# A transformer block's first stage: load order, look-ahead and ring of the adaLN modulation, its column sums by transposes, and the row scale applied once

## The chip, the cores and the metric

The kernel runs on one core of a Trainium2 chip. TensorE (PE) multiplies, VectorE (DVE) and ScalarE (ACT) do elementwise work, SyncE (SP) and GpSimd (POOL) issue DMA transfers from device memory. Each engine takes its instructions in the order in which the program lists them and waits on semaphores of the others. The metric is the device time of one execution in microseconds (us), lower is better; a kernel's time is the median of its runs.

## What is computed

One block of a diffusion transformer on 256 tokens `x` and 256 context tokens `ctx`, width 2048. What the change touches is its opening: two conditioning vectors are turned into a shift and a scale per column, the RMS-normed inputs are modulated by them, and the result is multiplied by the projection matrix.

```python
def adaln(cond, w, b):
    mod = jax.nn.silu(cond) @ w + b
    return mod.reshape(cond.shape[0], N_MOD, D_MODEL)

def modulate(x, gain, shift, scale):
    return rms_norm(x, gain) * (1 + scale[:, None, :]) + shift[:, None, :]
...
        mod_x = adaln(c, w_ada[l], b_ada[l])
        mod_c = adaln(c_ctx[None, :], w_ada[l], b_ada[l])
        pc = split_projection(modulate(ctx, norm1_g[l], mod_c[:, 0], mod_c[:, 1]) @ w_in[l])
        px = split_projection(modulate(x, norm1_g[l], mod_x[:, 0], mod_x[:, 1]) @ w_in[l])
```

Behind it come a gated linear recurrence in two directions, windowed attention, a merge and a feed-forward layer with a convolution. The change leaves those as they are.

## The kernel before

All activations lie transposed, 128 columns of the width on the partitions and 512 tokens (256 of `x`, 256 of `ctx`) along the free axis; the width is 16 such k-tiles (`KT`). `xraw` holds the raw inputs, `hl` the modulated ones, split into a high part `xhi` and a remainder `xlo` in the fast matmul format (fp32r), since every product is made as three fp32r products, high by high, high by low and low by high (`mm3`). Weights arrive as 512 KB pieces in `raw` (four buffers), ACT casts them to `whi` (L110), DVE takes the remainder `wlo` (L111).

**Head.** The modulation comes in eight *chunks* of two k-tiles; a chunk needs eight 512 KB pieces of the adaLN weight. They land in eight ring slots, four in the tile `ringv`, four in `ringq` (these are buffers of later stages that are still free). SP issues chunk 0's pieces with the four 1 MB loads of `xraw` among them, then those of chunk 1. ACT squares each k-tile of `xraw` (L203), PE adds the squares over the partitions with a matrix of ones (`bankm<-t,cst`), and ACT makes the row scale `rs` of it (L140, L141).

**One chunk.** `ada_mm` multiplies the conditioning vectors `csr` (32 columns, two of them used) with the pieces, in plain f32: 16 matmuls of 32x512 per chunk, and the k-th writes to the 32 output partitions 32*(k mod 4), so four neighbours use four different groups of the array's columns. The four partial sums lie on 128 partitions of one bank. `mod_chunk` copies that bank to `rows` (ACT, L180), and four small matmuls with a 0/1 matrix `sel` turn each 128-column piece upright and add the four partials (`banks<-sel,t`). DVE makes `bcol` and `acol`, shift and scale per column, out of it (L185 to L187). Then for each of two k-tiles: DVE multiplies `xraw` by `rs` (L190), ACT applies scale and shift, 256 tokens at a time (L193), ACT casts to `xhi` (L130), DVE takes `xlo` (L131).

**The loop.** `for j in range(8)`: iteration j multiplies the two k-tiles of chunk j with the value weights (`unit_v_mm`, 24 products, `bankm<-whi,hl` and `bankm<-wlo,hl`, inputs stationary) and with three tiles of the forget-gate weights (`unit_f_mm`, 18 products, `banks<-hl,whi` and so on). Among them it makes the modulation of chunk j+2: half of its `ada_mm` behind the value products, half behind the gate products, then `mod_chunk(j + 2)`. After the loop come the heads of q (`q_heads`), whose low products are 128x256, and the rest of the kernel.

What sets the order on each engine is a list scheduler that runs when the program is built: it starts from the order of the code, shifted by the priorities (`tc.high_priority`), and lets an instruction pass another when its own estimate says that the other isn't ready. The result is fixed; on the chip each engine keeps to it.

Of the kernel before, what the change touches and what calls it, by code (L numbers as in the profile page):

```python
# [27 lines left out]
RUSH = 120  # L28
# [23 lines left out]
def block_kernel(ctx, tc, xct, prm, cst, ada2, wst, out):  # L52
    nc = tc.nc
    V, S, PE = nc.vector, nc.scalar, nc.tensor

    cons = ctx.enter_context(tc.tile_pool(name="cons", bufs=1))
    big = ctx.enter_context(tc.tile_pool(name="big", bufs=1))
    strm = ctx.enter_context(tc.tile_pool(name="strm", bufs=3))
    scr = ctx.enter_context(tc.tile_pool(name="scr", bufs=3))
    tiny = ctx.enter_context(tc.tile_pool(name="tiny", bufs=8))  # L60
    mm = ctx.enter_context(tc.tile_pool(name="mm", bufs=5, space=bass.MemoryType.PSUM))
    ms = ctx.enter_context(tc.tile_pool(name="ms", bufs=3, space=bass.MemoryType.PSUM))

    def bank(pool=None):
        pool = pool or mm
        return pool.tile([P, 512], F32, name="bank" + ("m" if pool is mm else "s"))

    def mmul(o, l, r, start, stop):
        PE.matmul(o, l, r, start=start, stop=stop, skip_group_check=True)  # L69
# [69 lines left out]
    def rsqrt(dst, src, scale):  # L139
        S.activation(dst, src, AF.Ln, bias=eps_c, scale=scale)  # L140
        S.activation(dst, dst, AF.Exp, scale=-0.5)  # L141
# [22 lines left out]
    sel = smalltile(2, "sel")  # L164
    V.tensor_tensor(sel, ident[:, 0:2], ident[:, 32:34], op=ALU.add)
    V.tensor_tensor(sel, sel, ident[:, 64:66], op=ALU.add)
    V.tensor_tensor(sel, sel, ident[:, 96:98], op=ALU.add)
    rs = scr.tile([P, 512], F32, name="rs", bufs=1)

    def ada_load(i):  # L170
        st.load_raw(slots[i])

    def ada_mm(aps, half):
        for kt in range(8 * half, 8 * half + 8):
            g = 32 * (kt % 4)
            mmul(aps[g:g + 32, :], csr[:, kt, :], slots[kt // 2][:, kt % 2 * 512:kt % 2 * 512 + 512], kt < 4, kt >= KT - 4)

    def mod_chunk(j, aps):
        rows = scr.tile([P, 512], F32, name="t")
        S.copy(rows, aps)  # L180
# [4 lines left out]
        V.tensor_tensor(bcol[:, js, :], a4[:, 0:2, :], bsh[:, js, None].broadcast_to([P, 2, 2]), op=ALU.add)  # L185
        V.tensor_tensor(acol[:, js, :], a4[:, 2:4, :], bsc[:, js, None].broadcast_to([P, 2, 2]), op=ALU.add)
        V.tensor_tensor(acol[:, js, :], acol[:, js, :], par("n1g")[:, js, None].broadcast_to([P, 2, 2]), op=ALU.mult)  # L187
        for kt in range(2 * j, 2 * j + 2):
            hn = scr.tile([P, 512], F32, name="t")
            V.tensor_tensor(hn, xraw[:, kt, :], rs, op=ALU.mult)  # L190
            for cnd in range(2):
                sl = slice(T * cnd, T * cnd + T)
                S.activation(hn[:, sl], hn[:, sl], AF.Identity, bias=bcol[:, kt, cnd:cnd + 1],  # L193
                             scale=acol[:, kt, cnd:cnd + 1])
            split(xhi[:, kt, :], xlo[:, kt, :], hn)

    ssq = bank()

    def x_part(i):
        nc.sync.dma_start(xraw[:, 4 * i:4 * i + 4, :], xct[:, 4 * i:4 * i + 4, :])  # L200
        for kt in range(4 * i, 4 * i + 4):
            sq = scr.tile([P, 512], F32, name="t")
            S.activation(sq, xraw[:, kt, :], AF.Square)  # L203
            mmul(ssq, ones, sq, kt == 0, kt == KT - 1)

    for i in range(8):
        ada_load(i)
        if i % 2:
            x_part(i // 2)
    for j in range(2):  # L210
        if j:
            for i in range(8):
                ada_load(i)
        aps = bank(ms)
        for half in range(2):
            ada_mm(aps, half)
        with tc.high_priority(offset=0 if j else RUSH):
            if not j:
                rsqrt(rs, ssq, 1.0 / D)
            mod_chunk(j, aps)  # L220
    base[0] = tc.tile_snap_priority()
    early_v = [bank() for _ in range(4)]

# [19 lines left out]
    def unit_v(j):  # L243
        st.load()
        return [st.next(4) for _ in range(2)]

    def unit_v_mm(j, wv, tts):
        for tt in tts:
            ts = slice(tt * P, tt * P + P)
            for k2 in range(2):  # L250
                kt = 2 * j + k2
                mm3(early_v[tt], xhi[:, kt, ts], xlo[:, kt, ts], *wv[k2], kt == 0, kt == KT - 1)

    def unit_f(j):
        st.load(6)
        w = [st.next() for _ in range(6)]
        st.pos = 8
        return w

    def unit_f_mm(j, w):  # L260
        for b in range(3):
            for k2 in range(2):
                kt = 2 * j + k2
                mm3(early_f[b], *w[3 * k2 + b], xhi[:, kt, :], xlo[:, kt, :], kt == 0, kt == KT - 1)


    for j in range(8):
        more = j < 6
        aps = bank(ms) if more else None
        wv = unit_v(j)  # L270
        if more:
            for i in range(4):
                ada_load(i)
        unit_v_mm(j, wv, range(4))
        if more:
            ada_mm(aps, 0)
        w = unit_f(j)
        if more:
            for i in range(4, 8):
                ada_load(i)  # L280
        unit_f_mm(j, w)
        if more:
# [243 lines left out]
    kT = big.tile([P, 2, 512], F32, name="kT", tag="kT")  # L526
    va = big.tile([P, 4, 256], F32, name="va", tag="va")
# [50 lines left out]
    for h in range(H):  # L578
        if h == 4:
            bs = [bank() for _ in range(4)]  # L580
# [4 lines left out]
        if h == 6:  # L585
            bs = [bank() for _ in range(4)]
# [384 lines left out]
```

## Time and profile before

| | |
|---|---|
| Median of three runs | 1745.06 us (1742.27 to 1748.81) |
| The profiled execution's own time | 1748.49 us |
| Its span, first to last instruction | 1746.6 us |
| PE busy | 1719.9 us, 98% of the span |
| DVE, ACT, POOL busy | 1197.0, 847.6, 68.4 us |
| Mean granted TensorE clock | 0.996 of full |
| Bytes moved by DMA | 371.85 MB, mean 213 GB/s |

In rows of the timeline the first number is the start in us from the span's beginning, the second the time from the first start to the last end of the row's instructions, then engine, line, operation, what is written from what is read, shape, and how many instructions the row holds. A bracket at the end is the engine's idle time before the row and what ended it. A plain f32 matmul shows as two records (x8 is four matmuls), an fp32r product as one. In rows that give busy time by stretches, (x..) is the count, then PEclk is the granted clock, then the share of the DMA engines that was busy, then GB/s.

### The profile page before, as it was taken

The page shows a single profiled execution, that of the slowest core. Times are in us where ns is not written, and L with a number is a line of the kernel's source. Part 1 is how long each engine was busy: PE and PEld are TensorE (multiplying, and loading weights), DVE is VectorE, ACT ScalarE, POOL GpSimd, SP SyncE. Part 2 cuts the span into 40 slices and gives each one's busy share as a digit, 9 for nine tenths or more (in the row PEclk, how much of TensorE's full clock was granted, in tenths as well). Part 3 has the DMA queues.
Part 4 walks back from the last instruction along what each step waited for, and adds up shares of the span by engine and source line. Part 5 has one row for each costly group of instructions (what it writes and reads, how often), then busy time and mean ns, then how long its engine had stood idle before and what let it go on. Part 6 is the DMA issues. An engine that isn't in the chain of part 4 may idle for free.

```text
span 1746.6 us, 24907 instructions
## 1 busy us (share of the span) xinstructions
PE 1719.9 (98%) x9562; PEld 1451.9 (83%) x9562; DVE 1197.0 (69%) x1807; ACT 847.6 (49%) x1292; POOL 68.4 (4%) x132
## 2 busy tenths in 40 slices
PE   7999999999999999999999999999999999999999
PEld 2567888888888888888888898888888888888887
DVE  1335967464669878697878797788766656666665
ACT  4335554252545755454455475555555334554332
POOL 0000100000000001010100000000000000000000
PEclk9999999999999999999999999999999999999999
DMA  9795744433436558686876567677755555555554
GB/s 374 297 364 184 265 143 157 161 117 117 136 104 214 202 189 289 233 309 237 304 249 231 190 215 256 228 239 262 233 183 186 188 185 188 183 192 182 190 196 145
DMA packets 103432, 371.85 MB, mean 213 GB/s; under 512 B 11280, under 2 KB 13712, under 8 KB 102800
## 3 DMA queue, kind: packets, MB, share of 16 engines
q1 hardware_dynamic: 84880, 303.14, 49.2%
q0 software_dynamic: 18432, 67.12, 11.8%
q8 instruction: 75, 1.23, 0.3%
q14 instruction: 45, 0.37, 0.1%
HBM read 368.11 MB, written 2.10 MB: 212 GB/s over the span
## 4 chain that ended last, share of the span: by engine, by line
PE 93%; DMA 4%; DVE 1%; issue 1%; ACT 0%; SPq 0%; DVEq 0%; POOLq 0%
PE bankm L69 84%; PE banks L69 6%; DMA araw<-in_ada_dram 3%; DVE wlo L111 1%; PE banks L493 0%; DMA raw<-in_wst_dram 0%; DVE acc L309 0%; DMA xraw<-in_xct_dram 0%; PE banks L666 0%; PE banks L317 0%; PE banks L485 0%; PE banks L475 0%; PE banks L522 0%; ACT whi L110 0%; PE banks L636 0%
## 5 line engine op out<-in xcount | busy, mean ns | idle before, releaser
L69 PE MATMUL bankm<-hl,whi 128*128 128x512 f32 (+1 forms) x3392 | 1163.3, 394 | 0.0
L69 PE MATMUL bankm<-hl,wlo 128*128 128x256 f32 (+2 forms) x3104 | 899.7, 290 | 4.1 <-DVE wlo L111 4.1
L111 DVE TENSOR_TENSOR wlo<-raw,whi 128x1024 fp32r<-128x1024 f32 x498 | 606.7, 1219 | 337.2 <-ACT whi L110 335.1
L110 ACT CAST whi<-raw 128x1024 fp32r<-128x1024 f32 x498 | 520.2, 1045 | 634.8 <-PE bankm L69 492.5
L69 PEld LDWEIGHTS bankm<-hl,whi 128*128 128x128 f32 x3392 | 633.0, 188 | 144.1
L69 PEld LDWEIGHTS bankm<-hl,wlo 128*128 128x128 f32 x3104 | 587.6, 189 | 16.4 <-DVE wlo L111 5.7
L309 DVE SCALAR_TENSOR_TENSOR acc<-araw,csil,acc 128x1024 f32<-128x1024 f32 x120 | 153.7, 1281 | 29.4 <-DMA araw<-in_ada_dram 28.6
L69 PE MATMUL bankm<-whi,hl 128*128 128x512 f32 x512 | 167.3, 400 | 6.3 <-ACT whi L110 6.3
L69 PEld LDWEIGHTS bankm<-whi,hl 128*128 128x128 f32 x512 | 96.7, 190 | 31.3 <-ACT whi L110 7.2
L304 POOL DMA_DIRECT2D araw<-in_ada_dram x128 | 68.2, 533 | 1172.5 <-DVE acc L309 671.7
L69 PE MATMUL bankm<-wlo,hl 128*128 128x512 f32 x256 | 101.2, 395 | 0.0
L69 PE MATMUL bankm<-yb,whi 128*128 128x512 f32 x256 | 91.0, 400 | 0.0
L69 PE MATMUL bankm<-g,whi 128*128 128x512 f32 x256 | 90.5, 399 | 0.0
L69 PE MATMUL bankm<-yb,wlo 128*128 128x256 f32 x256 | 72.2, 282 | 0.0
L69 PE MATMUL bankm<-g,wlo 128*128 128x256 f32 x256 | 71.9, 281 | 0.0
L813 DVE SCALAR_TENSOR_TENSOR xm<-bankm,modv,xm 128x256 f32<-128x256 f32 x96 | 46.4, 484 | 31.2 <-PE bankm L69 29.4
L69 PEld LDWEIGHTS bankm<-g,whi 128*128 128x128 f32 x256 | 48.1, 188 | 12.0
L69 PEld LDWEIGHTS bankm<-yb,whi 128*128 128x128 f32 x256 | 48.1, 188 | 11.8
L69 PEld LDWEIGHTS bankm<-wlo,hl 128*128 128x128 f32 x256 | 48.6, 190 | 10.6 <-DVE wlo L111 1.2
L69 PEld LDWEIGHTS bankm<-yb,wlo 128*128 128x128 f32 x256 | 48.4, 189 | 0.3
L69 PEld LDWEIGHTS bankm<-g,wlo 128*128 128x128 f32 x256 | 48.4, 189 | 0.0
L793 ACT ACTIVATE fs<-fs,prm 128x256 f32<-128x256 f32 x44 | 26.5, 601 | 43.7 <-DVE fs L368 43.5
(200 smaller groups left out, 1187.4 us busy)
## 6 DMA issues: line engine op xcount, KB each, us to landing
raw<-in_wst_dram SPq DMA_DIRECT2D x490, 512.0 KB, 3.4
araw<-in_ada_dram POOLq DMA_DIRECT2D x128, 512.0 KB, 4.7
ringv<-in_wst_dram SPq DMA_DIRECT2D x32, 512.0 KB, 5.9
ringq<-in_wst_dram SPq DMA_DIRECT2D x32, 512.0 KB, 6.3
xraw<-in_xct_dram SPq DMA_DIRECT2D x4, 1024.0 KB, 12.8
raw<-in_wst_dram SPq DMA_DIRECT2D x8, 384.0 KB, 7.3
xm<-in_xct_dram SPq DMA_DIRECT2D x2, 1024.0 KB, 9.1
out_dram<-xm SPq DMA_DIRECT2D x3, 512.0 KB, 3.6
```

Of the source, the lines that this page charges most:

```text
L69: PE.matmul(o, l, r, start=start, stop=stop, skip_group_check=True)
L110: S.copy(hi, raw)
L111: self.last = V.tensor_tensor(lo, raw, hi.bitcast(F32), op=ALU.subtract)
L304: nc.gpsimd.dma_start(raw, ada2[idx])
L309: V.scalar_tensor_tensor(acc, raw, csil[:, kt, 0:1], acc, op0=ALU.mult, op1=ALU.add)
L793: S.activation(t, s, AF.Identity, bias=cb[:, f:f + 1], scale=cw[:, f, 1:2])
L813: V.scalar_tensor_tensor(xm[:, j, :], o[:, T * i:T * i + T], gate2[:, j:j + 1], xm[:, j, :], op0=ALU.mult, op1=ALU.add)
```

## The change

Five edits, all in the head and in the loop over eight chunks.

- **Loads.** The four loads of `xraw` come first, then only chunk 0's eight pieces, then the value and gate weights of iteration j ahead of the pieces of chunk j+1.
- **Look-ahead.** The head makes one chunk (0) instead of two. Iteration j makes chunk j+1: the first half of its `ada_mm` behind the value products, the second half behind the first of the three gate tiles, then `mod_chunk(j + 1)` at a raised priority, then the other two gate tiles.
- **Ring.** Three groups of four slots in place of two: `ringv`, `ringq`, and a spare group in two buffers of a later stream (`araw`) and two further tiles (`ringkT`, `ringva`). Half h of chunk j uses group (2j+h) mod 3.
- **Column sums.** The four matmuls with `sel` become four 128x128 transposes (L181), and one DVE reduction adds the four partials (L183).
- **Row scale.** All 16 k-tiles of `xraw` are multiplied by `rs` in place, once, in the head (L214). Per k-tile ACT then writes `xhi` straight from `xraw` (L192, 256 tokens at a time), DVE makes the same value in f32 in place (L193) and takes `xlo` (L194). The separate cast to `xhi` is gone.

```diff
-    slots = [r[:, i, :] for r in ring for i in range(4)]
+    spare = [strm.tile([P, 1024], F32, name="araw", bufs=2) for _ in range(2)]
+    spare += [big.tile([P, 1024], F32, name="ring" + t, tag=t) for t in ("kT", "va")]
+    slots = [[r[:, i, :] for i in range(4)] for r in ring] + [spare]
...
+    def ada_load(j, half):
+        for slot in slots[(2 * j + half) % 3]:
+            st.load_raw(slot)
...
         for q in range(4):
-            mmul(aps[:, 2 * q:2 * q + 2], rows[:, q * P:q * P + P], sel, q == 0, True)
-        a4 = aps[:, 0:8].rearrange("p (q c) -> p q c", c=2)
+            PE.transpose(aps[:, q * P:q * P + P], rows[:, q * P:q * P + P], ident)
+        m8 = smalltile(8).rearrange("p (q c) -> p q c", c=2)
+        V.tensor_reduce(m8, aps.rearrange("p (q g c) -> p q c g", q=4, g=4)[:, :, 0:2, :], axis=AX.X, op=ALU.add)
...
         for kt in range(2 * j, 2 * j + 2):
-            hn = scr.tile([P, 512], F32, name="t")
-            V.tensor_tensor(hn, xraw[:, kt, :], rs, op=ALU.mult)
             for cnd in range(2):
-                sl = slice(T * cnd, T * cnd + T)
-                S.activation(hn[:, sl], hn[:, sl], AF.Identity, bias=bcol[:, kt, cnd:cnd + 1],
-                             scale=acol[:, kt, cnd:cnd + 1])
-            split(xhi[:, kt, :], xlo[:, kt, :], hn)
+                xs = xraw[:, kt, T * cnd:T * cnd + T]
+                a, b = acol[:, kt, cnd:cnd + 1], bcol[:, kt, cnd:cnd + 1]
+                S.activation(xhi[:, kt, T * cnd:T * cnd + T], xs, AF.Identity, bias=b, scale=a)
+                V.tensor_scalar(xs, xs, a, b, op0=ALU.mult, op1=ALU.add)
+            V.tensor_tensor(xlo[:, kt, :], xraw[:, kt, :], xhi[:, kt, :].bitcast(F32), op=ALU.subtract)
...
-    for i in range(8):
-        ada_load(i)
-        if i % 2:
-            x_part(i // 2)
-    for j in range(2):
...
+    for i in range(4):
+        x_part(i)
+    aps = bank(ms)
+    for half in range(2):
+        ada_load(0, half)
+        ada_mm(aps, 0, half)
+    with tc.high_priority(offset=RUSH):
+        rsqrt(rs, ssq, 1.0 / D)
+        for kt in range(KT):
+            V.tensor_tensor(xraw[:, kt, :], xraw[:, kt, :], rs, op=ALU.mult)
+        mod_chunk(0, aps)
...
     for j in range(8):
-        more = j < 6
+        wv, w = unit_v(j), unit_f(j)
+        more = j < 7
         aps = bank(ms) if more else None
...
+        for half in range(2 * more):
+            ada_load(j + 1, half)
         unit_v_mm(j, wv, range(4))
         if more:
-            ada_mm(aps, 0)
...
+            ada_mm(aps, j + 1, 0)
+        unit_f_mm(j, w, (0,))
         if more:
-            ada_mm(aps, 1)
-            mod_chunk(j + 2, aps)
+            ada_mm(aps, j + 1, 1)
+            with tc.high_priority(offset=24):
+                mod_chunk(j + 1, aps)
+        unit_f_mm(j, w, (1, 2))
```

The host packs the weights in the new order, and both kernels issue the same number of matmuls for products and modulation. From six products ahead of the end of the loop on, PE's list is the same in both kernels; DVE's and ACT's differ up to the first heads of the recurrence and are the same from there.

On PE, before, around the end of one iteration and the start of the next (the first five iterations read so): `ringq,csr` is the second half of a chunk's modulation, `whi,hl` and `wlo,hl` are value products of the next iteration, `sel,t` the column sums.

```order
L69 MATMUL bankm<-hl,wlo 128x512
L69 MATMUL banks<-ringq,csr 32x512 x8
L69 MATMUL bankm<-whi,hl 128x512
L69 MATMUL bankm<-wlo,hl 128x512
L69 MATMUL bankm<-whi,hl 128x512 x2
L69 MATMUL banks<-sel,t 128x2 x4
```

Eight modulation matmuls stand together, and the chunk that is summed here is used a whole iteration later. The same place in the changed kernel, from the end of iteration 4 on (the modulation's pieces lie in `ringkT` and `ringva` here; `hl,whi` and `hl,wlo` are the last gate products of the iteration, `cst,t` are the transposes):

```order
L69 MATMUL banks<-ringkT,csr 32x512 x2
L69 MATMUL banks<-hl,whi 128x512
L69 MATMUL banks<-hl,wlo 128x512
L69 MATMUL bankm<-hl,whi 128x512
L69 MATMUL banks<-ringva,csr 32x512 x2
L69 MATMUL bankm<-hl,whi 128x512
L69 MATMUL bankm<-hl,wlo 128x512
L69 MATMUL bankm<-hl,whi 128x512 x2
L181 MATMUL banks<-cst,t 128x128 x4
L69 MATMUL bankm<-hl,wlo 128x512
L69 MATMUL bankm<-whi,hl 128x512 x2
L69 MATMUL bankm<-wlo,hl 128x512 x2
```

The modulation now stands in pieces of one to four matmuls with products between them, and one product behind the transposes the next iteration's value products begin, which read the very chunk that is being summed. From its first value product to the first 128x256 product of `q_heads`, PE's list of before holds 92 modulation matmuls in 12 runs (one of 4, eleven of 8); that of the change holds 111 in 32 runs: 7, 8, 8, 8, 2, 6, 6, 2, and then four times 1, 3, 4, 4, 2, 2.

On DVE, the head of the change (the first k-tiles of `xlo` follow further down; L226 and L227 are small steps of the gate's lower bounds):

```order
L214 TENSOR_TENSOR xraw<-xraw,rs 128x512 x16
L183 TENSOR_REDUCE tn<-banks 128x8
L226 TENSOR_TENSOR tn<-prm 128x16
L111 TENSOR_TENSOR wlo<-raw,whi 128x1024
L185 TENSOR_TENSOR acol<-tn,bsc 128x4
L187 TENSOR_TENSOR bcol<-tn,prm 128x4
L227 TENSOR_TENSOR tn<-prm,tn 128x16
L186 TENSOR_TENSOR acol<-acol,prm 128x4
```

Before, the three small steps L185 to L187 came first and two k-tiles of L190 behind them; now all 16 row-scale passes and one weight remainder stand ahead of chunk 0's shift and scale. On SP, the first loads of the change:

```order
L82 DMA prm<-in_prm_dram 128x635
L83 DMA cst<-in_cst_dram 128x256
L199 DMA xraw<-in_xct_dram 128x2048 x4
L117 DMA ringv<-in_wst_dram 128x1024 x4
L117 DMA ringq<-in_wst_dram 128x1024 x4
L109 DMA raw<-in_wst_dram 128x1024
```

Before, 22 pieces of the modulation and the four loads of `xraw` stood ahead of the first `raw`; now eight pieces do.

More of the change, by code (lines that the diff above doesn't have):

```diff
@@ L162, in block_kernel, with ada_mm @@
     V.tensor_copy(csr[:, :, 0:2], csil)
[L164 to L167, printed above, removed]
     rs = scr.tile([P, 512], F32, name="rs", bufs=1)
-    def ada_load(i):
-        st.load_raw(slots[i])
-    def ada_mm(aps, half):
+    def ada_load(j, half):
+        for slot in slots[(2 * j + half) % 3]:
+            st.load_raw(slot)
+    def ada_mm(aps, j, half):
         for kt in range(8 * half, 8 * half + 8):
-            g = 32 * (kt % 4)
-            mmul(aps[g:g + 32, :], csr[:, kt, :], slots[kt // 2][:, kt % 2 * 512:kt % 2 * 512 + 512], kt < 4, kt >= KT - 4)
+            g, c = 32 * (kt % 4), kt % 2 * 512
+            mmul(aps[g:g + 32, :], csr[:, kt, :], slots[(2 * j + half) % 3][kt % 8 // 2][:, c:c + 512], kt < 4, kt >= KT - 4)
     def mod_chunk(j, aps):
@@ L181, in mod_chunk @@
         for q in range(4):
-            mmul(aps[:, 2 * q:2 * q + 2], rows[:, q * P:q * P + P], sel, q == 0, True)
-        a4 = aps[:, 0:8].rearrange("p (q c) -> p q c", c=2)
+            PE.transpose(aps[:, q * P:q * P + P], rows[:, q * P:q * P + P], ident)
+        m8 = smalltile(8).rearrange("p (q c) -> p q c", c=2)
+        V.tensor_reduce(m8, aps.rearrange("p (q g c) -> p q c g", q=4, g=4)[:, :, 0:2, :], axis=AX.X, op=ALU.add)
         js = slice(2 * j, 2 * j + 2)
-        V.tensor_tensor(bcol[:, js, :], a4[:, 0:2, :], bsh[:, js, None].broadcast_to([P, 2, 2]), op=ALU.add)
-        V.tensor_tensor(acol[:, js, :], a4[:, 2:4, :], bsc[:, js, None].broadcast_to([P, 2, 2]), op=ALU.add)
+        V.tensor_tensor(acol[:, js, :], m8[:, 2:4, :], bsc[:, js, None].broadcast_to([P, 2, 2]), op=ALU.add)
         V.tensor_tensor(acol[:, js, :], acol[:, js, :], par("n1g")[:, js, None].broadcast_to([P, 2, 2]), op=ALU.mult)
+        V.tensor_tensor(bcol[:, js, :], m8[:, 0:2, :], bsh[:, js, None].broadcast_to([P, 2, 2]), op=ALU.add)
         for kt in range(2 * j, 2 * j + 2):
-            hn = scr.tile([P, 512], F32, name="t")
-            V.tensor_tensor(hn, xraw[:, kt, :], rs, op=ALU.mult)
             for cnd in range(2):
-                sl = slice(T * cnd, T * cnd + T)
-                S.activation(hn[:, sl], hn[:, sl], AF.Identity, bias=bcol[:, kt, cnd:cnd + 1],
-                             scale=acol[:, kt, cnd:cnd + 1])
-            split(xhi[:, kt, :], xlo[:, kt, :], hn)
+                xs = xraw[:, kt, T * cnd:T * cnd + T]
[3 more added lines that the diff above has]
+            V.tensor_tensor(xlo[:, kt, :], xraw[:, kt, :], xhi[:, kt, :].bitcast(F32), op=ALU.subtract)
     ssq = bank()
@@ L204, in x_part @@
             mmul(ssq, ones, sq, kt == 0, kt == KT - 1)
-    for i in range(8):
-        ada_load(i)
-        if i % 2:
-            x_part(i // 2)
-    for j in range(2):
[L211 to L220, printed above, removed]
+    for i in range(4):
[9 more added lines that the diff above has]
+        mod_chunk(0, aps)
     base[0] = tc.tile_snap_priority()
@@ L258, in unit_f, with unit_f_mm @@
         return w
-    def unit_f_mm(j, w):
-        for b in range(3):
+    def unit_f_mm(j, w, bs):
+        for b in bs:
             for k2 in range(2):
@@ L921 @@
     first = np.stack([fft[0], fbt[0], fft[1]], 0).transpose(1, 0, 2, 3)
-    parts = [ada1[0], ada1[1]]
+    parts = [ada1[0]]
     for j in range(8):
-        more = ada1[j + 2] if j < 6 else ada1[0:0, 0]
-        parts += [vh[0, j][None], more[0:4]]
         t6 = first[2 * j:2 * j + 2].reshape(6, P, P)
-        parts += [_halves(np, np.concatenate([t6, np.zeros((2, P, P), np.float32)], 0)), more[4:8]]
+        parts += [vh[0, j][None], _halves(np, np.concatenate([t6, np.zeros((2, P, P), np.float32)], 0))]
+        if j < 7:
+            parts.append(ada1[j + 1])
     parts.append(_halves(np, qt))
```

9 lines of the change are left out of this document (removed).

## The prediction

> **What bounds the kernel now.** I read the page first (busy shares, then the chain that ended last), then busy time by stretches cut at the first product of the loop over chunks (47.7 us) and at its end (157.7 us), then the timeline of the first 80 us.
>
> ```profile
> span 1746.6 us, 24907 instructions
> PE 1719.9 (98%) x9562; PEld 1451.9 (83%) x9562; DVE 1197.0 (69%) x1807; ACT 847.6 (49%) x1292; POOL 68.4 (4%) x132
> PE 93%; DMA 4%; DVE 1%; issue 1%; ACT 0%; SPq 0%; DVEq 0%; POOLq 0%
> ```
>
> PE is the bound: 98% busy, and 93% of the chain that ended last is its own work. So a change pays if it starts PE's long run earlier or takes work off PE, and costs if it gives PE more to do or lets it wait.
>
> ```profile
> 0.00:47.70 47.70, 31.06 (x121) 10.88 (x121) 7.96 (x31) 21.77 (x39) 0.20 (x4) 0.98 0.96 378
> 47.70:157.70 110.00, 109.26 (x569) 73.69 (x570) 39.27 (x67) 43.12 (x68) 0.66 (x1) 0.98 0.76 283
> 157.70:215.00 57.30, 55.42 (x326) 48.13 (x326) 52.01 (x84) 33.98 (x57) 6.33 (x12) 0.97 0.75 254
> 215.00:1746.60 1531.60, 1524.17 (x8550) 1319.20 (x8548) 1097.71 (x1629) 748.75 (x1130) 61.21 (x115) 1.00 0.59 201
> ```
>
> The columns are stretch, length, then busy time of PE, PEld, DVE, ACT, POOL, clock, DMA share, GB/s. The head is bound by DMA: 96% of the engines busy, 378 GB/s, PE idle for 16.6 us. The loop is bound by PE: 109.26 of 110.00 us busy, with DMA at 76%. Behind the loop PE's list is unchanged and PE idles for 1.9 and 7.4 us, so what the loop's end gains or loses, the kernel's end gains or loses. Two questions remain: when does the first product of the loop start, and how long does the loop take?
>
> **The head.** These rows carry it:
>
> ```profile
> 9.93 1.67 ACT L203 ACTIVATE t<-xraw 128x512 f32<-128x512 f32 x3 [5.16 <-DMA xraw<-in_xct_dram]
> 10.61 5.74 PE L69 MATMUL bankm<-t,cst 128*128 128x512 f32 x8 [1.56 <-ACT t L203]
> ...
> 31.11 0.69 ACT L140 ACTIVATE rs<-bankm,prm 128x512 f32<-128x512 f32 x1 [1.95 <-PE bankm L69]
> ...
> 32.63 0.63 ACT L141 ACTIVATE rs<-rs 128x512 f32<-128x512 f32 x1
> ...
> 34.35 1.29 DVE L190 TENSOR_TENSOR t<-xraw,rs 128x512 f32<-128x512 f32 x2
> ...
> 38.56 0.42 SPq L109 DMA_DIRECT2D raw<-in_wst_dram  x1
> ...
> 46.59 1.04 ACT L110 CAST whi<-raw 128x1024 fp32r<-128x1024 f32 x1 [2.72 <-DMA raw<-in_wst_dram]
> 47.66 1.23 DVE L111 TENSOR_TENSOR wlo<-raw,whi 128x1024 fp32r<-128x1024 f32 x1 [3.08 <-ACT whi L110]
> ...
> 47.69 1.22 PE L69 MATMUL bankm<-whi,hl 128*128 128x512 f32 x2 [6.32 <-ACT whi L110]
> ```
>
> The first weight is issued at 38.56 us, behind 22 modulation pieces, lands at 46.59, and PE starts at 47.69 after 6.32 us of waiting. The change puts eight pieces ahead of that weight: with the inputs 9.4 MB, 25 us at 378 GB/s. So the weight is no longer late. Next late is the chain from the inputs to chunk 0. The first input load had a 0.52 MB piece ahead of it; without that it lands 1.4 us earlier, first square at 8.5, first sum on PE at 9.2. The first four sums take 5.74 us (to 14.9); the other twelve take 3.63 us per four (22.74 to 26.37 in the rows below), to 25.8. L140 and L141 take 0.69 and 0.63: `rs` at 27.2. Chunk 0's pieces (8.85 MB, 23.4 us of transfer) and its 16 matmuls end at about 30, so they are not late. But DVE now makes all 16 row-scale passes first. Two take 1.29 us, so 16 take 10.3: 37.6. Then L183 (taken as 0.2), the weight remainder that stands before the shift and scale (1.23), the small steps to ACT's start (0.45, rows below) and ACT's first 256 tokens (1.58 for three, 0.53): the first product starts at 40.0. **Gain 7.7 us.** Bounds: 6.3 if the inputs land no earlier than before; 15.7 if the row-scale passes were off the path (a rival).
>
> **The modulation's matmuls.** On PE a product's pace, and what an interruption by modulation costs:
>
> ```profile
> 150.26 0.39 PE L69 MATMUL bankm<-wlo,hl 128*128 128x512 f32 x1
> 150.49 0.62 PE L69 MATMUL bankm<-whi,hl 128*128 128x512 f32 x2
> 150.94 0.39 PE L69 MATMUL bankm<-wlo,hl 128*128 128x512 f32 x1
> ```
>
> ```profile
> 55.40 0.39 PE L69 MATMUL bankm<-whi,hl 128*128 128x512 f32 x1
> 55.72 1.07 PE L69 MATMUL banks<-ringv,csr 128*32 128x512 f32 x8
> 56.72 0.73 PE L69 MATMUL banks<-hl,whi 128*128 128x512 f32 x2
> 57.28 0.39 PE L69 MATMUL banks<-hl,wlo 128*128 128x512 f32 x1
> ```
>
> ```profile
> 75.38 0.39 PE L69 MATMUL bankm<-hl,wlo 128*128 128x512 f32 x1
> 75.69 1.92 PE L69 MATMUL banks<-ringq,csr 128*32 128x512 f32 x16
> 77.55 0.50 PE L69 MATMUL bankm<-whi,hl 128*128 128x512 f32 x1
> 77.89 0.40 PE L69 MATMUL bankm<-wlo,hl 128*128 128x512 f32 x1
> ```
>
> Three products take 0.68 us, 0.227 each. From 55.40 to 57.28 lie three products and a run of four modulation matmuls: 1.88 - 0.68 = 1.20 us for the run. From 75.38 to 77.89 lie two products and a run of eight: 2.51 - 0.45 = 2.06. What does a run of fewer than four cost? Two places in the head tell it:
>
> ```profile
> 21.76 1.05 PE L69 MATMUL banks<-ringq,csr 128*32 128x512 f32 x4
> 22.74 3.70 PE L69 MATMUL bankm<-t,cst 128*128 128x512 f32 x8
> ...
> 26.37 1.06 PE L69 MATMUL banks<-ringq,csr 128*32 128x512 f32 x8
> 27.37 3.70 PE L69 MATMUL bankm<-t,cst 128*128 128x512 f32 x8
> ```
>
> Two matmuls (x4 records) hold PE for 0.98 us, four for 1.00. Neighbours that write to different groups of 32 partitions run side by side, so a run costs by rounds of four, begun ones included. That speaks against the change, whose order cuts the runs up. Before: one run of four and eleven of eight, 1.20 + 11 x 2.06 = 23.9 us. After: six runs of 6 to 8, two rounds each (12.4), and 26 of at most four, taken at 1.20 like the run of four (31.2): 43.6. **Cost 19.7 us**, of which 4.1 is the chunk that moved from the head into the loop. A single matmul shows nowhere; if short runs cost the 1.00 of the head rows, the term is 14.5.
>
> **The column sums.**
>
> ```profile
> 78.60 0.95 PE L69 MATMUL banks<-sel,t 128*128 128x2 f32 x8
> 79.41 0.47 PE L69 MATMUL bankm<-wlo,hl 128*128 128x512 f32 x1
> ...
> 137.08 1.05 PE L69 MATMUL banks<-sel,t 128*128 128x2 f32 x8 [0.71 <-ACT t L180]
> ...
> 269.33 0.27 PE L475 MATMUL banks<-cst,hb 128*128 128x128 f32 x1
> 269.44 0.27 PE L317 MATMUL banks<-cst,acc 128*128 128x128 f32 x1
> ```
>
> The four `sel` matmuls cost 0.81 us, six times in the loop, with one wait of 0.71: 5.6 us. Transposes of this shape start 0.11 us apart; four take 0.44, between that and 0.81 with a change of format, and I take 0.6, seven times: 4.2. **Gain 1.4 us.** The Trainium skill (TensorE: Matmul & The Clock Gate, Part 4: PE-mode transpose) gives some 275 ns for a transpose in a kernel. The row's duration agrees (0.27) but its spacing is 0.11; by 275 ns in sequence the seven groups would cost about 4.6 us more by my estimate, and the sum would be 1765. The trace decides for the spacing.
>
> **The wait that is new.** Before, a chunk was ready an iteration ahead. Now, in the last four iterations with modulation, the transposes stand one product from the iteration's end, and the next product reads the chunk.
>
> ```profile
> 40.17 0.15 DVE L185 TENSOR_TENSOR bcol<-banks,prm 128x4 f32<-128x4 f32 x1
> ...
> 40.42 0.16 DVE L187 TENSOR_TENSOR acol<-acol,prm 128x4 f32<-128x4 f32 x1
> ...
> 40.62 1.58 ACT L193 ACTIVATE t<-t,bcol,acol 128x256 f32<-128x256 f32 x3 [1.82 <-DVE acol L187]
> ```
>
> ```profile
> L318 DVE TENSOR_REDUCE modv<-banks 128x4 f32<-128x512 f32 x16 | 10.9, 684 | 8.6 <-PE banks L317 8.6
> ```
>
> From the first transpose: the fourth ends at 0.6; 0.1 to DVE; the reduction of 32 elements, between a tiny step (0.15) and the 512 of L318 (0.68), taken as 0.2; the small steps 0.45; ACT's first 256 tokens 0.53: `xhi` at 1.9. PE is through at 0.6 + 0.23. It waits 1.1 us, with the whole of its list queued behind. Four times: **cost 4.4 us** (up to 6.3 with the long reduction). In the first three iterations five to eight products, or a run, stand behind the transposes and cover it. The remainder is hidden: L193 and L194 come due only behind two runs and nine products of PE, the prefetch of twelve slots runs a chunk and a half ahead at 5.1 MB per iteration, under what 378 GB/s brings in 14 us. ACT loses a 0.6 us cast per k-tile that nobody waited for.
>
> **Sum:** -7.7 + 19.7 - 1.4 + 4.4 = +15 us. The profiled execution of before took 1748.49 us, so the like of it would take 1763.5; it lies 3.4 above the median of 1745.06, so I forecast a median of 1760.
>
> **Rivals.**
> - *Runs cost by their matmuls, not by rounds.* If the array lets a lone piece run beside the products, 111 matmuls cost 2.06/8 = 0.257 each, 28.5 against 23.6: +4.9 in place of +19.7. Then the sum is about zero and the time 1745: not slower. It decides in the short runs; the kernel breaks even when one costs 0.63 us in place of 1.20. For it: no single piece shows in the trace. Against: two hold PE as long as four. The Trainium skill (same page, Part 3: Packing small matmuls) has the span of a pack grow by some 4 ns per tile, so that one costs nearly what four cost; by that, and the trace agrees, this rival gets only 0.13.
> - *The change does in the head what its words say, and no more:* `xhi` follows the loads, at 32 us, because the row-scale passes run beside other work. Gain 15.7: 1752. Against: DVE's order has all 16 ahead of L183. 0.07.
> - *The new wait doesn't arise*, because ACT and DVE are quicker than the 0.83 us of cover: 1756. Against: three dependent DVE steps and one of ACT. 0.13.
> - *The four input loads share the engines and land together*, at 4.65 MB or 14 us, in place of one after the other: the sums start 5.5 us later, 1766. For it: nothing stands between them any more. Against: before, the first square started at 9.93, when only some of what had been issued could be in. 0.08.
>
> **The numbers.** The forecast itself gets 0.57. The remaining 0.02 is a gain that I don't see. A measurement of this kernel can tell about 0.5%, 8.7 us, from no change. Slower by more than that: the forecast, the shared loads and half of the case without the wait, 0.72. Faster by more than that: the unseen gain, and 0.03 for costs by matmuls together with a missing wait and an earlier head, 0.05. Within: the rest, 0.23. Range 1749 to 1768: the low end takes in the earlier head, no wait, and short runs at 1.00 us; the high end the shared loads and the long reduction. Left out are the costs by matmuls and the unseen gain, with some tails 0.2. DVE's order also differs in the first 57 us behind the loop; PE idled 1.9 us there, which bounds what that can give.
>
> **What would show it.** In the profile of the change: the first product near 40 us, with PE waiting on ACT, and DVE's 16 L214 rows from 27 to 38 us ahead of it; single modulation matmuls that hold PE for about 1.2 us; four waits of PE on ACT L192 of about 1.1 us; the first 128x256 product near 173 us in place of 157.7. The forecast is wrong if the first product starts before 34 us, or if runs of one to three matmuls cost under 0.8 us.

## The result: 1763.5 us, 1.0% slower, and the profile after

| | before | after |
|---|---|---|
| Median | 1745.7 us (1742.27 to 1748.81, 4 runs) | 1763.47 us (1760.72 to 1765.7, 4 runs) |
| Ratio to before, 95% interval | | 1.0101, 1.0077 to 1.0125 |
| The profiled execution, its span | 1748.49, 1746.6 | 1765.7, 1763.6 |
| First product of the loop | 47.69 | 39.05 |
| The loop, to the first 128x256 product | 110.05 | 133.27 |
| From there to the end of the span | 1588.86 | 1591.28 |

The forecast was 1760 in a range of 1749 to 1768, and slower. A second measurement of the same kernel beside the experiments gave 1763.24 us and a ratio of 1.0090 (1.0069 to 1.0111).

The head of the page after, with the chain that ended last:

```profile
span 1763.6 us, 24861 instructions
PE 1731.5 (98%) x9530; PEld 1447.0 (82%) x9530; DVE 1206.3 (68%) x1844; ACT 838.5 (48%) x1276; POOL 68.7 (4%) x132
PE 85%; DMA 6%; DVE 5%; issue 4%; ACT 0%; SPq 0%; POOL 0%; DVEq 0%; POOLq 0%
```

PE is busy 11.6 us longer with 32 matmul records fewer, and idle for 32.1 us in place of 26.7. Both kinds of loss are there: more time inside PE's work, and more waiting. (Its share of the last chain fell from 93% to 85%; that says by which way the chain ran, here more often through DMA, and not how much time was lost.) Busy time by stretches, cut where the stretches of before were cut (the loop's first product and its end, then the same length behind it):

```profile
0.00:39.05 39.05, 22.05 (x71) 8.41 (x71) 12.61 (x32) 15.55 (x27) 0.20 (x4) 0.94 0.90 345
39.05:172.50 133.45, 128.78 (x589) 71.04 (x590) 45.10 (x102) 38.69 (x64) 0.00 (x0) 0.98 0.70 266
172.50:230.00 57.50, 56.96 (x338) 49.08 (x337) 52.55 (x84) 35.67 (x59) 7.03 (x13) 1.00 0.76 257
230.00:1763.60 1533.60, 1523.67 (x8537) 1318.47 (x8535) 1096.03 (x1628) 748.56 (x1128) 61.49 (x115) 1.00 0.59 201
```

The head gives 8.6 us, the loop takes 23.2, the rest takes 2.4: +17.0 on the span. The loop's PE is 4.67 us idle where before it was 0.74, and DMA has slack (0.70), and its long waits there name ACT, so it is not the loads that hold it.

The head, in the timeline of after:

```profile
8.52 1.67 ACT L202 ACTIVATE t<-xraw 128x512 f32<-128x512 f32 x3 [3.91 <-DMA xraw<-in_xct_dram]
...
25.60 0.69 ACT L140 ACTIVATE rs<-bankm,prm 128x512 f32<-128x512 f32 x1 [1.95 <-PE bankm L69]
...
26.98 9.72 DVE L214 TENSOR_TENSOR xraw<-xraw,rs 128x512 f32<-128x512 f32 x16 [21.93 <-ACT rs L141]
...
36.62 0.19 DVE L183 TENSOR_REDUCE tn<-banks 128x8 f32<-128x32 f32 x1
36.80 1.22 DVE L111 TENSOR_TENSOR wlo<-raw,whi 128x1024 fp32r<-128x1024 f32 x1
...
38.41 2.06 ACT L192 ACTIVATE hl<-xraw,bcol,acol 128x256 fp32r<-128x256 f32 x4
39.05 0.80 PE L69 MATMUL bankm<-whi,hl 128*128 128x512 f32 x1 [3.62 <-ACT hl L192]
```

Sixteen row-scale passes lie between the row scale and the first reduction, and PE's first product ends its wait on ACT. Then PE around one single modulation matmul and, a little later, around one group of transposes:

```profile
87.27 0.65 PE L69 MATMUL bankm<-whi,hl 128*128 128x512 f32 x2
87.76 0.66 PE L69 MATMUL bankm<-wlo,hl 128*128 128x512 f32 x2
88.35 1.04 PE L69 MATMUL banks<-araw,csr 128*32 128x512 f32 x2
89.33 0.50 PE L69 MATMUL bankm<-whi,hl 128*128 128x512 f32 x1
89.67 0.40 PE L69 MATMUL bankm<-wlo,hl 128*128 128x512 f32 x1
...
103.91 0.60 PE L181 MATMUL banks<-cst,t 128*128 128x128 f32 x4
104.27 0.48 PE L69 MATMUL bankm<-hl,wlo 128*128 128x512 f32 x1
105.89 0.74 PE L69 MATMUL bankm<-whi,hl 128*128 128x512 f32 x2 [1.14 <-ACT hl L192]
```

From 87.27 to 89.67 lie five products and one modulation matmul: 2.40 - 5 x 0.227 = 1.26 us for the one, no less than the 1.20 of a run of four. Ahead of it, though, the products start 0.24 to 0.27 us apart here. From the last product before it, which starts at 88.02 (the second of the x2 row), to the second behind it at 89.67 it is 1.64 - 2 x 0.227 = 1.19, and so it is at the three other single matmuls (1.18 to 1.19). The four transposes take 0.36 from their start to the next product's. And behind them PE waits for the chunk. The wait prints as 1.14, but the product behind a group of transposes has 0.31 to 0.32 to the next (85.56 to 85.87 at the group before), so from 104.27 the following one was due at some 104.59 and started at 105.89: 1.30 us lost. The same wait of 1.14 or 1.15 stands at 124.60, 143.26 and 161.93.

### The profile page after: what moved, and what is told of

The parts are those of the page before. It is cut to its first block, busy times and chain, and to the rows that moved or that the text cites. A ratio compares the mean times of both kernels' runs of the same rounds, so it can differ in the third digit from the quotient of the medians.

```text
span 1763.6 us, 24861 instructions
## 1 busy us (share of the span) xinstructions
PE 1731.5 (98%) x9530; PEld 1447.0 (82%) x9530; DVE 1206.3 (68%) x1844; ACT 838.5 (48%) x1276; POOL 68.7 (4%) x132
## 4 chain that ended last, share of the span: by engine, by line
PE 85%; DMA 6%; DVE 5%; issue 4%; ACT 0%; SPq 0%; POOL 0%; DVEq 0%; POOLq 0%
PE bankm L69 76%; PE banks L69 7%; DMA araw<-in_ada_dram 5%; DVE wlo L111 2%; DVE acc L301 1%; DVE xraw L214 1%; PE banks L485 0%; PE banks L467 0%; PE banks L658 0%; DMA xraw<-in_xct_dram 0%; PE banks L477 0%; PE banks L309 0%; ACT hl L192 0%; DVE t L360 0%; PE banks L181 0%
## 5 line engine op out<-in xcount | busy, mean ns | idle before, releaser
L69 PEld LDWEIGHTS bankm<-wlo,hl 128*128 128x128 f32 x256 | 48.5, 191 | 10.3 <-DVE wlo L111 1.1
L183 DVE TENSOR_REDUCE tn<-banks 128x8 f32<-128x32 f32 x8 | 1.5, 191 | 79.1 <-ACT whi L110 64.9
```

The costliest lines, as they stand in the source:

```text
L183: V.tensor_reduce(m8, aps.rearrange("p (q g c) -> p q c g", q=4, g=4)[:, :, 0:2, :], axis=AX.X, op=ALU.add)
```

## The experiments

The theory (*by rounds*): the loop lost because a run of modulation matmuls costs by its begun rounds of four, and the new order cuts 12 runs into 32; on top comes the wait for the chunk; the head's gain is bounded by the row-scale passes. The rival (*by number*): runs cost 0.257 us per matmul, however cut, and the loss comes from something else. All kernels compute the whole reference. In the diffs, `behind(i)` makes what is inside it come after instruction i in the built order.

**The runs made whole again.** `whole_runs` is the changed kernel with this loop:

```python
+            with behind(*[last_of[tt] for tt in range(4)]):   # last value products
+                ada_mm(aps, j + 1, 0)
+        with behind(last_of["mm"]):                           # last matmul issued
+            unit_f_mm(j, w, (0,))
...
+            with behind(last_of["mm"]):
+                ada_mm(aps, j + 1, 1)
...
+        with behind(last):                                    # the second run's last
+            unit_f_mm(j, w, (1, 2))
```

> The changed kernel with nothing altered but PE's order in the loop: the modulation comes in 14 whole runs of eight, and the transposes stand four products behind the second run, so that eight or more products follow them before the next iteration reads the chunk. By rounds: 14 x 2.06 = 28.8 us in place of 32 runs with 43.6, so -14.8, and the four waits of 1.14 us are gone, -4.6: together -19.4 and a time near 1744, not to be told from the kernel before although the first product still starts at 39. By number of matmuls (0.257 each, 112 in place of 111): the runs give nothing, the waits at most -4.6: 1759 or more.

Measured: 1749.53 us (12 runs), 1.0018 of before (1.0003 to 1.0034): 14 us under the changed kernel, where rounds with the waits gone gave 19.4. Its loop:

```profile
39.70:158.85 119.15, 114.58 (x589) 71.64 (x590) 45.57 (x102) 39.24 (x65) 0.20 (x1) 0.97 0.78 297
```

PE's busy time in the loop fell by 14.0 (128.59 in the exact stretch of after, 39.05 to 172.32), where the rounds gave 14.8 and the number of matmuls nothing: the rival is out for the runs. But PE is still idle for 4.6 us, the waits did not go. That the medians differ by 14 as well is partly chance: the two profiled executions lie 20.1 apart, 14.1 in the loop and 6.7 behind it, where the changed kernel has a wait that is treated below, and the twelve runs of `whole_runs` go from 1745.1 to 1755.6. Where eight products follow the transposes, PE, ACT and DVE show:

```profile
83.79 0.60 PE L189 MATMUL banks<-cst,t 128*128 128x128 f32 x4
...
87.65 0.50 PE L71 MATMUL bankm<-whi,hl 128*128 128x512 f32 x1 [1.41 <-ACT hl L200]
```

```profile
82.92 0.59 ACT L187 COPY t<-banks 128x512 f32<-128x512 f32 x1 [10.26 <-PE banks L71]
83.41 1.79 ACT L118 CAST whi<-raw 128x1024 fp32r<-128x1024 f32 x2
87.00 2.08 ACT L200 ACTIVATE hl<-xraw,bcol,acol 128x256 fp32r<-128x256 f32 x4 [1.80 <-DVE acol L194]
```

```profile
84.50 0.19 DVE L191 TENSOR_REDUCE tn<-banks 128x8 f32<-128x32 f32 x1 [10.26 <-ACT whi L118]
84.61 2.09 DVE L119 TENSOR_TENSOR wlo<-raw,whi 128x1024 fp32r<-128x1024 f32 x2
86.62 0.15 DVE L193 TENSOR_TENSOR acol<-tn,bsc 128x4 f32<-128x4 f32 x1
```

The reduction is done at 84.7, the next step needs 0.15 us and comes at 86.62: DVE makes the remainders of two weight tiles in between. The other chunks of the same run tell the same. In the first two no remainder stands among the steps (reduction at 69.97, next step at 70.19, for one), and PE waits at most 0.07 us; where the remainders stand behind the small steps it waits 0.5, where they stand ahead of them 1.4. The chain is not as short as its own steps; it is as long as what stands among them on two engines that keep their order.

**The row scale, when a chunk's turn comes.** `whole_late` is `whole_runs` with two row-scale passes ahead of chunk 0 in place of sixteen:

```python
     def mod_chunk(j, aps):
+        with behind(*[last_of["chunk"]] if j else []):   # last remainder of chunk j-1
+            for kt in range(2 * j, 2 * j + 2):
+                V.tensor_tensor(xraw[:, kt, :], xraw[:, kt, :], rs, op=ALU.mult)
...
-        for kt in range(KT):
-            V.tensor_tensor(xraw[:, kt, :], xraw[:, kt, :], rs, op=ALU.mult)
         mod_chunk(0, aps)
```

> whole_runs, and the row-scale passes of a chunk made only when that chunk's turn comes: two passes instead of sixteen stand ahead of the first reduction. If the row-scale passes are what holds the first product, it starts at about 31.5 us in place of 39.05 (rs at 26.95, two passes to 28.3, but the transposes end only at 30.3; then 0.2 for the reduction, 0.45 for the small steps, 0.55 for ACT), and the whole comes out 7.5 us under whole_runs, near 1737, faster than both kernels. Rival: the weights are what sets the start or the pace, because the loop would now end at about 146 us and the loads ahead of that need some 337 GB/s on the mean: then the gain of the head is given back in the loop as waits for raw, and the time stays near 1744.

Measured: 1741.99 us (12 runs), 0.9972 of before (0.9958 to 0.9986), 7.5 under `whole_runs`, as expected from that; the absolute figure of 1737 was missed by the waits that stayed. The first product starts at 32.66 (expected 31.5) in place of 39.70, and the loop is 118.02 long (119.15 in `whole_runs`). The rival, weights as the pace, has little: one wait of 0.19 us for a ring slot, with DMA at 0.84. So the fourteen passes that chunk 0 doesn't need cost the changed kernel 7 us of its head.

**The reverse: cutting the kernel before.** `before_uncut` writes PE's order in the middle of each iteration out (run of eight, 18 products, run of eight); `before_cut` and `before_cut1` differ from it in one table alone, which says ahead of which of the 18 products which matmuls stand:

```python
+    CUT = {0: (0, range(8)), 18: (1, range(8))}                        # before_uncut
+    CUT = {0: (0, (0, 1)), 2: (0, (2, 3)), 4: (0, (4, 5)), 6: (0, (6, 7)),
+           12: (1, (0, 1)), 14: (1, (2, 3)), 16: (1, (4, 5)), 18: (1, (6, 7))}   # before_cut
+    CUT = {**{i: (0, (i,)) for i in range(8)}, **{11 + i: (1, (i,)) for i in range(8)}}   # before_cut1
```

> The control: the kernel before with PE's order in the middle of each iteration written out (run of eight, 18 products, run of eight), as it nearly was already; four matmuls of the first chunk move from the head into the loop. Every theory: within 2 us of the kernel before.

> The control with each run of eight cut into four pieces of two matmuls, two products between pieces: 48 pieces in place of 12 runs, the same matmuls and products, no other change. By rounds: a piece costs what a run of four costs, 1.20, so 4.8 in place of 2.06 per run, 12 times: +33 us against the control, 1.9%. By number of matmuls: nothing, at most +5 from changing over oftener (36 more changes at up to 0.15).

> before_cut with pieces of one matmul: 96 single matmuls, a product between each two. In before_cut a piece of two takes 1.19 us of PE (from one piece to the next 1.64, less two products). If a begun round is what is paid, a piece of one takes the same 1.19: 96 x 1.19 = 114 in place of 12 x 2.06 = 24.7, +89 us against the control, 1839. If what is paid is a change-over (0.83) and 0.15 per matmul, which fits pieces of two and runs of eight as well, it takes 0.98: +69, 1819. By number of matmuls alone: no more than 1755.

Measured: the control 1749.53 us (12 runs), 1.0021 of before (1.0008 to 1.0034), that is 4 to 5 us where 2 were allowed, and its loop is 2.7 longer: the four matmuls that moved into it account for 0.9, waits for 1.2. Pieces of two: 1776.6 us, 1.0168 (1.0149 to 1.0188), 27 over the control for 33 expected by rounds. Pieces of one: 1831.6 us, 1.0492 (1.0473 to 1.0512), 82 over it for 89. Part of what is missing is in the control, whose loop has 1.9 us of waits that the cut ones have not; and of the profiled execution of pieces of two, the loop is 29.7 us longer than the control's, but what stands behind it, with PE's list unchanged, 4.3 shorter. The loops of the three:

```profile
48.39:161.11 112.72, 110.81 (x577) 74.24 (x578) 39.13 (x67) 43.07 (x68) 0.66 (x1) 0.98 0.74 279
```

```profile
47.83:190.29 142.46, 142.42 (x577) 73.39 (x578) 38.82 (x67) 42.83 (x68) 0.66 (x1) 0.98 0.64 220
```

```profile
45.78:243.42 197.64, 197.59 (x578) 82.04 (x578) 38.81 (x67) 42.53 (x68) 0.66 (x1) 0.99 0.47 158
```

The same 577 or 578 matmul records keep PE busy for 110.8, 142.4 and 197.6 us. Per run of eight that is 31.6 / 12 = 2.63 and 86.8 / 12 = 7.23 more than its 2.06, so a piece of two costs 4.69 / 4 = 1.17 and a piece of one 9.29 / 8 = 1.16. One matmul costs what two cost, and what a run of four costs (1.20). That is the begun round; the change-over with a price per matmul, which gave 0.98 for one, is out as well. A fixed price of each run is in it all the same: a second round adds only 2.06 - 1.20 = 0.86, so by estimate some 0.34 of the 1.20 goes with the interruption, and the 14.8 of `whole_runs` are 8.6 for ten rounds fewer and 6.1 for 18 interruptions fewer.

**Eight ring slots in place of twelve.** `two_groups` is the changed kernel without the third group of slots:

```python
-    slots = [[r[:, i, :] for i in range(4)] for r in ring] + [spare]
+    slots = [[r[:, i, :] for i in range(4)] for r in ring]
...
-        for slot in slots[(2 * j + half) % 3]:
+        for slot in slots[half]:
...
```

> The changed kernel with eight ring slots in place of twelve (the third group of four dropped). The order of PE then cuts fewer runs: 23 runs, ten of two rounds and thirteen of one. By rounds: 10 x 2.06 + 13 x 1.20 = 36.2 in place of 43.6, -7.4, and two of the four short leads go, though the waits stay as in whole_runs: near 1756. If the four more slots carry the loads over something, PE waits for ring DMA and that gain is lost: 1763 or more. By number of matmuls: no change from the runs, 1763.

Measured: 1758.19 us (6 runs), 1.0065 of before (1.0047 to 1.0083), 5 under the changed kernel, and no wait of PE for a ring slot: the four more slots carry nothing over here. The loop is 125.15 long, 8.1 less than that of after, for 7.4 by rounds and two waits fewer (2.6), less a new wait of 1.0 for a weight remainder. The first product came later, at 40.97, for another reason than in the changed kernel:

```profile
40.97 1.22 PE L69 MATMUL bankm<-whi,hl 128*128 128x512 f32 x2 [10.04 <-ACT whi L110]
```

Here the first weight is issued at 30.62 behind six of chunk 1's pieces, where after issues it at 17.29, and its cast stands behind the chunk's shift and scale on ACT. That takes back 1.9 us.

**More lead for the chunk.** `early_runs` is `whole_late` with the runs of the second iteration twelve products earlier, by which those of all later ones move too (the first run stands behind 12 value products, the second behind 6 more):

```python
+        early_run = 0 < j < 7
+        unit_v_mm(j, wv, range(2) if early_run else range(4))
...
+            if early_run:
+                unit_v_mm(j, wv, (2,))
...
+        if early_run:
+            with behind(last):
+                unit_v_mm(j, wv, (3,))
+                unit_f_mm(j, w, (0,))
```

> whole_late with the two whole runs moved twelve products forward from the second iteration on, so that the transposes stand 20 products ahead of the next iteration in place of 8. In whole_runs and whole_late PE still waits 0.5 to 1.4 us at each chunk, though eight products follow the transposes: DVE and ACT have the next weights' casts and remainders (1.05 and 1.2 us each) in the same stretch as the chunk's reduction and shift and scale. If that collision is what holds PE, 2.7 us more of lead end it: about -3.5 us, a time near 1738.5. Rival: the casts are bound to the chunk by the engines' order and not by time, so that they move with it: nothing changes, 1742. A second rival: the runs now come before their pieces have landed, and PE waits for the ring's DMA instead: 1742 or more.

Measured: 1732.8 us (6 runs), 0.9918 of before (0.9902 to 0.9934): the fastest kernel of the study, 13 us under before and 30 under the changed kernel, and 9 under `whole_late`, where 3.5 were expected. Its loop is 112.76 long, 5.3 less. From the start of the second iteration on PE has no wait for a chunk but the 1.41 and 0.47 us there. Against `whole_late`, DVE's order up to the last chunk has not changed:

```profile
74.02 0.19 DVE L194 TENSOR_REDUCE tn<-banks 128x8 f32<-128x32 f32 x1 [7.74 <-ACT whi L118]
74.24 0.16 DVE L196 TENSOR_TENSOR acol<-tn,bsc 128x4 f32<-128x4 f32 x1
...
74.52 1.22 DVE L119 TENSOR_TENSOR wlo<-raw,whi 128x1024 fp32r<-128x1024 f32 x1
75.66 0.41 DVE L204 TENSOR_SCALAR xraw<-xraw,acol,bcol 128x256 f32<-128x256 f32 x1
75.99 0.96 DVE L119 TENSOR_TENSOR wlo<-raw,whi 128x768 fp32r<-128x768 f32 x1
...
78.56 0.69 DVE L205 TENSOR_TENSOR hl<-xraw,hl 128x512 fp32r<-128x512 f32 x1
```

The remainders still stand among the chunk's steps, and 5.2 us pass from the reduction to the last `xlo`; but the transposes (73.31) now lie 20 products ahead of the next iteration, and PE does not wait. Part of the surplus is a wait that I had read too small. In `whole_late` the product at an iteration's start reads:

```profile
65.92 0.40 PE L71 MATMUL bankm<-wlo,hl 128*128 128x512 f32 x1
66.86 0.73 PE L71 MATMUL bankm<-whi,hl 128*128 128x512 f32 x2 [0.54 <-DVE hl L205]
```

The page counts 0.54 from the modelled end of the product before; from start to start it is 0.94 where 0.23 is the pace, so 0.71. The six such waits come to 4.3; less the 0.5 of the new one that is 3.8 of the loop's 5.3. The rest, 1.5 in the loop, 0.7 in the head and 3.5 behind the loop, belongs to no edit that I can name; waits for `wlo` behind the loop fell from 4.0 to 1.9.

**The changed kernel once more,** unaltered:

> The changed kernel once more, beside the others. Its profiled execution had one wait of 3.2 us for DVE behind the loop (hb L440), which no other kernel shows. If that wait belongs to the changed order of DVE there, it comes again; if it is chance, it is gone and the span behind the loop's end is near 1588 or less in place of 1591. The time should be within 3 us of 1763.5 either way.

Measured: 1763.24 us (4 runs). The wait came again, 3.3 us, and the stretch behind the loop is 1591.11 long, so it is not by chance. In after it reads:

```profile
253.25 1.97 PE L69 MATMUL banks<-hb 128*128 128x128 f32 x8 [3.19 <-DVE hb L440]
```

```profile
238.21 1.28 DVE L301 SCALAR_TENSOR_TENSOR acc<-araw,csil,acc 128x1024 f32<-128x1024 f32 x1 [2.37 <-DMA araw<-in_ada_dram]
...
244.14 1.29 DVE L301 SCALAR_TENSOR_TENSOR acc<-araw,csil,acc 128x1024 f32<-128x1024 f32 x1 [2.31 <-DMA araw<-in_ada_dram]
245.34 1.22 DVE L111 TENSOR_TENSOR wlo<-raw,whi 128x1024 fp32r<-128x1024 f32 x1
246.48 0.55 DVE L422 TENSOR_SCALAR hb<-hb,lb_t 128x512 f32<-128x512 f32 x1
```

DVE stands for two pieces of a later modulation before it comes to the recurrence's steps, on which PE waits. `two_groups` has the wait too (2.2 us), the kernels with whole runs don't. What moves it was not tested. The wait costs more than its length. The granted clock (third column from the right) of after around it:

```profile
250.00:253.25 3.25, 0.06 (x1) 0.00 (x0) 3.22 (x10) 3.22 (x8) 0.00 (x0) 0.95 0.04 18
253.25:256.00 2.75, 2.75 (x13) 2.75 (x14) 2.74 (x4) 1.43 (x3) 0.00 (x0) 0.50 0.58 197
256.00:259.00 3.00, 3.00 (x11) 2.52 (x10) 0.78 (x2) 1.70 (x3) 0.00 (x0) 0.50 0.48 178
```

At half clock the same matmuls fall behind those of before by 3.1 us more, on top of 3.4 for the wait.

## Why the prediction was right, step by step

Measured are the differences of the two profiled executions.

| step | forecast | measured | from |
|---|---|---|---|
| Head | -7.7 | -8.6 | first product 39.05 for 40.0 |
| Runs | +19.7 | +20.6 | what the loop's +23.2 leaves when the next rows are taken off |
| Column sums | -1.4 | -3.1 | 7 x 0.36 for 5.6 |
| The new wait | +4.4 | +5.2 | 4 x 1.30 |
| Clock at the loop's start | not named | +0.5 | first 24 products 8.49 for 8.03 |
| Behind the loop | none (within 1.9) | +2.4 | 1591.28 for 1588.86 |
| Sum | +15 | +17.0 | spans |

- *The head* held in its chain, link by link: first square at 8.52 (forecast 8.5), `rs` at 26.95 (27.2), the sixteen passes 9.72 us (10.3), the first product 39.05. That they are the bound is shown by `whole_late`, which starts at 32.66. The rival in which they lie beside other work is out; so is that of the shared loads, since the first square was 1.4 us earlier, not later.
- *The runs* were the decisive step, and the one where the trace of before had no row for a single matmul. I took it at 1.20, like a run of four. The rows after say 1.19, the reverse test 1.16. Counted from product to product, the 32 runs cost 43.6, the figure of the forecast; so of the +20.6 in the table, which is what is left over, about 0.9 is not the runs and has no place. The rival with costs by number (0.13) is out from both sides: 32 runs made into 14 gave 14.0 of PE's time back, and the same matmuls cut up cost the kernel before 27 and 82 us.
- *The wait* came where it was forecast, four times, and from the transposes to the product took 1.98 us for a forecast of 1.9. In the first three iterations it was covered, as forecast (0.08 us at 57.50 is all). What I had wrong is the reason: I took five to eight products behind the transposes to be enough. In `whole_runs` eight were not in five of seven iterations, because DVE and ACT have up to 2.1 us of weight work queued among the chunk's steps; 20 were.
- *The sums* were over-priced: transposes take 0.36 as a group, and I had added a change of format that is not in that spacing. 1.7 us too little gain.
- *Behind the loop* I bounded the effect by PE's idle time in the first 57 us, 1.9. Both ways it went further. By 218 us the change was 2.5 us ahead of before, counted from the loop's end: 1.0 by less waiting, and some 1.6 because before has a stretch at half clock there that the change has not:

```profile
203.00:206.00 3.00, 3.00 (x11) 2.54 (x11) 3.00 (x6) 1.76 (x3) 0.53 (x2) 0.52 0.75 258
```

Then came the wait at 253 us, outside the window that I had looked at, with 3.4 and the 3.1 of its half clock; 1.5 came back by the end. PE's list was unchanged throughout, DVE's waits for DMA were not. So the +2.4 is the small rest of larger terms that the prediction put at nothing.

Head and sums came out 2.6 better than forecast; runs, wait, clock and the stretch behind came out 4.6 worse. The errors have both signs, and what is left is 2 us on the span: the mechanisms of head, runs and wait held, and that the total is as close as 2 us is in part luck.

## What to carry to other kernels

A price for small matmuls that share the array holds for the whole pack: before an order spreads them, count begun packs in the order that was built and not matmuls, and keep each pack together. A chain that runs through two engines is as long as all that stands among its steps there, so give it lead by that length. A wait of PE can cost about its length twice, as the one at 253 us does: once as a wait and once as half clock behind it. The version that beats both kernels keeps the change's loads and sums, and takes back only what it did to the order: whole runs, the row scale when a chunk's turn comes, the chunk 20 products ahead.

## What the runs showed of the hardware

TensorE's clock set part of the time between the head and the loop and behind some waits, which no step of the prediction named. Granted clock (third column from the right) around the first product, in after and in `whole_late`:

```profile
34.00:39.05 5.05, 1.43 (x3) 0.11 (x3) 4.57 (x15) 0.76 (x3) 0.00 (x0) 0.55 1.02 415
39.05:42.00 2.95, 2.93 (x6) 1.94 (x7) 2.84 (x6) 2.26 (x5) 0.00 (x0) 0.50 1.02 417
42.00:45.00 3.00, 3.00 (x9) 2.30 (x9) 2.63 (x7) 1.05 (x1) 0.00 (x0) 0.55 1.03 421
45.00:48.00 3.00, 3.00 (x18) 2.00 (x20) 0.00 (x0) 0.31 (x1) 0.00 (x0) 1.00 0.86 344
```

```profile
32.66:36.00 3.34, 3.32 (x13) 2.33 (x14) 3.34 (x10) 1.64 (x5) 0.00 (x0) 1.00 0.98 380
36.00:39.00 3.00, 3.00 (x17) 2.10 (x17) 1.75 (x5) 0.83 (x1) 0.00 (x0) 1.00 1.03 418
```

In after PE did one matmul between 30.5 and 39.05; the clock was at half when the products came and stayed so for some 6 us, so that six to nine products fit into 3 us in place of thirteen to eighteen. In `whole_late`, where PE had idled 1.41 us, it stayed at 1.00, and the first 24 products took 6.0 us (32.66 to 38.67) for 8.5. The Trainium skill (TensorE: Matmul & The Clock Gate, Part 1: The HAM clock gate) has the clock fall to half after an idle window of about 3.4 us and rise after as long a busy one, with windows that run freely and don't start with the work. The rise took 5.7 us of work here (39.05 to 44.7), which a window that was already running can explain. The fall behind the head agrees; other falls came with less idle time. The wait of 3.2 us at 253 us was enough, and so was one of 2.2 us: in `two_groups` PE waits until 245.23, and its clock reads 0.50 from 246.7 to 250.0. In before the clock falls at some 202.5, and none of PE's waits in the 44 us from the loop's end to there is over 0.9. So these runs give no length of wait that is safe.

Before had the same half clock (0.50 from 47.69 to 52), so it nearly cancels between the two kernels. In `whole_late`, whose first 24 products took 2.7 us less than those of `whole_runs` (6.01 for 8.68), an earlier start was worth more than its own length over these products; the whole loop came out 1.1 shorter.
